# Memory heads' P times V at 512 columns, a pinned weight cast, and shifted loads and steps in a two-layer encoder kernel

## The chip, the core and the metric

The kernel runs on one core of one Trainium2 chip. A core has several engines that run side by side, each with its own queue of instructions: TensorE (PE in the profile; PEld is its loading of the stationary operand), VectorE (DVE), ScalarE (ACT), GpSimd (POOL) and SyncE (SP), which here issues most of the DMA transfers. Engines wait for one another through semaphores. On-chip memory has 128 partitions; matmuls write to eight banks of an accumulation memory (PSUM), each 128 x 512 fp32. The metric is the device time of one run in microseconds (us); the median of several runs counts.

## What is computed

Two layers (DEPTH = 2), sequence 512, width 2048, batch 1. Each layer normalises x, projects it, and runs three groups of heads side by side: eight heads of latent attention (MLA) over 512 keys, a short gated convolution, and four memory heads, which attend to 256 memory tokens. The outputs are gated, projected back, normalised and added to x. The parts that matter here:

```python
def memory_attention(q, mem_n, w_mk, w_mv):
    mk = (mem_n @ w_mk).reshape(b, m, MEM_HEADS, MEM_HEAD_DIM)      # 256 keys, 4 heads of 128
    mv = (mem_n @ w_mv).reshape(b, m, MEM_HEADS, MEM_HEAD_DIM)
    sc = einsum('bshd,bmhd->bhsm', q, mk) * MEM_HEAD_DIM ** -0.5
    p = softmax(sc, axis=-1)
    o = einsum('bhsm,bmhd->bshd', p, mv)

for l in range(DEPTH):
    z = rmsnorm(x, pre_norm_g[l]) @ w_in[l]
    q_lat, kv_lat, k_pe, gb, gc, xin, q_mem, gate = split_cols(z)
    q = rmsnorm(q_lat, ...) @ w_uq[l]            # the MLA heads' q, then rope on 64 columns
    k_nope, v = split(rmsnorm(kv_lat, ...) @ w_ukv[l])
    a_out = mla_attention(q, k, v)
    c_out = short_gated_conv(gb, gc, xin, conv_w[l])
    m_out = memory_attention(q_mem, rmsnorm(mem, ...), w_mk[l], w_mv[l])
    o = (concat(a_out, c_out, m_out) * silu(gate)) @ w_o[l]
    x = x + rmsnorm(o, post_norm_g[l])
```

## The kernel before

**Products in three parts.** Every fp32 operand is split into a high half, rounded to the matmul's own 32-bit type, and a low half, the rest. `mm3` (lines 267 to 269) makes a product of three matmuls: high times high, high times low, low times high. `split_to` (272 and 273) makes the halves of a result: ScalarE copies it (the cast), VectorE subtracts.

**Weights.** `Program` keeps a list of steps; a step names the weight units that it reads. A unit is loaded by SP into one of eight raw buffers (`wr`) and prepared in two instructions: a ScalarE cast to `wh` (184) and a VectorE subtraction to `wl` (185), each in one of three buffers. With `parts=2` each is done in two halves, so that the first half is there sooner. Loads are issued some eight units ahead, preparations two units ahead of their step.

**What sets the order.** TensorE, GpSimd and SP run in the order in which the program was written. ScalarE and VectorE are ordered by the framework's scheduler, except in the first stretch of the kernel, up to the memory keys of layer 1, where they too keep program order.

**The start.** Layer 1 begins with the memory tokens' keys and values: sixteen steps (`mem_steps`) that alternate keys and values for eight slices `kp` of the width, 256 rows of `w_mk` or `w_mv` each. The operands `mH`, `mL` are the memory tokens, transposed ahead of time. Twelve matmuls on ones (`warm(12)`, line 1372) stand ahead of them. The table `beside` names what else is put behind each of the sixteen steps: loads of x rows (`xr[t][0]`), their squares (`xr[t][1]`), loads of the transposed x (`load`), and its multiplications by the norm's gains on ScalarE (`gain`, line 687). All loads are on SP's queue.

**The mixer.** `mixer` runs the heads of a layer. Each head has four steps, one for each 128 queries: `score` (three matmuls, the row maximum on VectorE at 1126, the exponential on ScalarE at 1129, reciprocal at 1131, normalised P on ScalarE at 1132), `trans` (TensorE transposes at 1142 to `ptp`, then a cast and a subtraction to the halves of `PT`), and `av`, the product of P and V into `o`. `pipeline` writes them out: step k issues `score` of iteration k, then what `between` holds for k, then `trans` of iteration k - 3, and `av` of iteration k - 5 (k - 4 for the whole MLA heads). The four memory heads come first (iterations 0 to 15), then four pairs of MLA heads. In an MLA head `av` runs once, 512 queries wide, with the slabs `PTh` and `PTl`. In a memory head it runs twice, for 256 queries each, from a slab `PT` for each half:

```python
if t % 2 == 0:
    st["PT"] = slab("PT", F32R).rearrange("p (s k c) -> p s k c", s=2, k=4)
...
o = st["o"] if whole else st["o"][:, b * 256:(b + 1) * 256]
```

**Between.** `qkv_steps` are the six projections that a pair of MLA heads needs: two of q (`qps`), two of k (`kps`), two of v (`vps`); the weight units are `uq` and `ukv`. `spread` distributes the six over the steps of the heads that run before that pair: the first pair's over the sixteen steps of the memory heads, another pair's over the eight steps of the pair before it, save that those of the fourth pair are put within six of the third pair's eight steps. `pair2` holds what is added in the third pair: `use_y` and two casts of gated outputs y, `low(0)` and `low(1)`, at steps 6, 6 and 7.

Of the kernel before, what the change touches and what calls it, by code (L numbers as in the profile page):

```python
# [5 lines left out]
F32 = mybir.dt.float32  # L6
F32R = mybir.dt.float32r
# [56 lines left out]
class Unit:  # L64
# [5 lines left out]

    def __init__(self, key, loads=None, more=None, sums=(), then=(), place=None, alloc=None, gain=None, parts=1, behind=None):
        self.key = key
        self.loads = loads or {}
        self.more = more
        self.sums, self.then = sums, then
        self.place = place
        self.alloc = alloc
        self.gain = gain
        self.parts = parts
        self.behind = behind  # L80


class Program:
    def __init__(self, nc, raw, hi, lo, ahead=2, loads_ahead=6, more_ahead=5):
        self.nc = nc
        self.pools = raw, hi, lo
        self.ahead, self.loads_ahead, self.more_ahead = ahead, loads_ahead, more_ahead
        self.steps = []
        self.early = 0
        self.queue = []  # L90
# [32 lines left out]
    def run(self):  # L123
# [39 lines left out]
        def prep(upto):  # L163
            while at["prep"] < min(upto, len(seq)):
# [5 lines left out]
                u = seq[c]  # L170
                src = tiles[u.key]
                for a, b in u.sums:
                    nc.vector.tensor_tensor(tiles[a], tiles[a], tiles[b], op=ALU.add)  # L173
# [7 lines left out]
                if u.gain is None:  # L181
                    for k in range(u.parts):
                        h = slice(k * n // u.parts, (k + 1) * n // u.parts)
                        nc.scalar.copy(hi[:, h], src[:, h])  # L184
                        nc.vector.tensor_tensor(lo[:, h], src[:, h], hi[:, h].bitcast(F32), op=ALU.subtract)  # L185
                else:
                    gains = u.gain()
                    for k, g in enumerate(gains):
                        h = slice(k * (n // len(gains)), (k + 1) * (n // len(gains)))
                        nc.scalar.activation(hi[:, h], src[:, h], AF.Copy, scale=g)  # L190
                        nc.vector.scalar_tensor_tensor(lo[:, h], src[:, h], g, hi[:, h].bitcast(F32),
                                                       op0=ALU.mult, op1=ALU.subtract)
# [30 lines left out]
def encoder(tc, x, xt, mem, memt, positions, columns, w_in, q_norm_g, w_uq, w_qr, kv_norm_g, w_ukv,  # L223
# [18 lines left out]
    dram = pool("dram", space=bass.MemoryType.DRAM)  # L242
    pr = Program(nc, raw_p, hi_p, lo_p)
    add = pr.add
# [539 lines left out]
    def mem_steps(l):  # L784

        def unit(name, w, kp):
            if (l, kp) == (0, 0):
                return Unit((name, l, kp), {(name, l, kp): [w[j * P:(j + 1) * P, :] for j in range(2)]}, parts=2)
            return Unit((name, l, kp), {(name, l, kp): [w[kp * 256:(kp + 1) * 256, :].rearrange("(a p) c -> p a c", p=P)]})

# [252 lines left out]
    def qkv_steps(l, pair, st):  # L1043
# [3 lines left out]
        qu = Unit(qk, {qk: [wl[:, :, 2 * pair + i, :NOPE] for i in range(2)]})  # L1047
        ku = Unit(kk, {kk: [wkv[:, :, pair * 512:(pair + 1) * 512]]})

# [48 lines left out]
    def head_iters(j, rope, src, keys, whole=False):  # L1098
# [4 lines left out]
        def room(t):  # L1103
            if whole:
                if t == 0:
                    st["PT"] = [slab(n, F32R).rearrange("p (k c) -> p k c", k=kts) for n in ("PTh", "PTl")]
                sl = slice(t * P, (t + 1) * P)
                return [a[:, :, sl] for a in st["PT"]]
            if t % 2 == 0:
                st["PT"] = slab("PT", F32R).rearrange("p (s k c) -> p s k c", s=2, k=4)  # L1110
            sl = slice((t % 2) * P, (t % 2 + 1) * P)
            st["PT", t // 2] = [st["PT"][:, s, :kts] for s in range(2)]
            return [a[:, :, sl] for a in st["PT", t // 2]]
# [32 lines left out]
        def av(b):  # L1146
            def g():
# [10 lines left out]
            return g  # L1158
        return [((score(t), [], 0.4), trans(t), av(t // 2) if t == 3 or t == 1 and not whole else None, 4 if whole else 5)
                for t in range(NT)]  # L1160
# [10 lines left out]
    def mem_head(i):  # L1171
        def src():
# [3 lines left out]
                    (lambda k: V[:, 0, k, ds], lambda k: V[:, 1, k, ds]))  # L1176
        return head_iters(12 + i, None, src, MT)

# [24 lines left out]
    def mixer(l, C, gates, pair2, tail):  # L1203
# [16 lines left out]
        for pair in range(4):  # L1220
            for i in range(2):
                its += mla_head(2 * pair + i, sts[pair])
            nxt = tail if pair == 3 else spread(6 if pair == 2 else 8, qkv_steps(l, pair + 1, sts[pair + 1]),
                                                0.0 if pair else 0.25)
# [171 lines left out]
    add(row_load("x", x[0], 0))  # L1396
    add(lambda: warm(12))
    G["src"], G["dst"] = x[0], None
    for l in range(depth):
# [7 lines left out]
        if l == 0:  # L1407
# [20 lines left out]
            def load(h, g):  # L1428
# [4 lines left out]
            beside = {  # L1433
                0: [xr[1][0]], 2: [load(0, 0)], 4: [xr[0][1]], 5: [xr[1][1], load(0, 1)],
                6: [wide_of(0), gain(0, 0, 0, 2)], 7: [gain(0, 0, 2, 6)], 8: [gain(0, 0, 6, 8), row_of(0)],
                9: [scaled(0, 0, 0), gain(0, 1, 0, 4), mr[0][0]], 10: [left_part(0, 0, 0)],
# [116 lines left out]
        if l + 1 < depth:  # L1553
            add(lambda: G.update(mTd=dram.tile([4, P, D], F32, name="mTd")))
        mixer(l, C, gates, {6: [(use_y, []), (low(0), [])], 7: [(low(1), [])]}, last_pair)
        add(sums(1))
# [56 lines left out]
```

## Time and profile before

| | |
|---|---|
| median of 3 runs | 1476.92 us (1476.54 to 1476.97) |
| profiled execution, its own time | 1476.71 us |
| its span in the trace | 1474.9 us |
| mean granted TensorE clock | 0.999 |
| DMA | 288.93 MB, mean 196 GB/s |
| longest group by line | ScalarE's weight casts, line 184: 434 instructions, 445.4 us |

The span runs from the first to the last recorded instruction; the execution's own time is 1.8 us longer. In the profile's rows of a timeline stand start, duration, engine, line, operation, output and inputs, shape, count, and in brackets the idle time before the instruction with what ended it. In rows of groups the numbers behind the first bar are the busy time in us and the mean duration in ns, behind the second the idle time. In rows by windows, the window and its length come first, then the busy us and the number of instructions of PE, PEld, DVE, ACT and POOL, the granted clock, the DMA share and GB/s. Matmuls overlap in their pipeline: the duration of one is longer than the time from its start to the next one's.

### The profile page before, as it was taken

How to read it: one execution, taken by the hardware profiler on the slowest of the kernel's cores; microseconds unless marked ns; L12 is line 12 of the kernel's file. 1: busy time of each engine (PE TensorE's matmuls, PEld its weight loads, DVE VectorE, ACT ScalarE, POOL GpSimd, SP SyncE). 2: the span in 40 equal slices, each digit the busy share in tenths (PEclk: the TensorE clock that was granted, in tenths of full speed). 3: DMA queues.
4: the chain of work that ended last, by engine and by line, in shares of the span. 5: the costliest groups of instructions: out<-in, count | busy, mean ns of one | idle time of the engine just before them, and what ended most of it. 6: DMA issues, size and time to landing. Idle time of an engine off the chain costs nothing.

```text
span 1474.9 us, 19573 instructions
## 1 busy us (share of the span) xinstructions
PE 1462.4 (99%) x7250; PEld 1251.1 (85%) x7250; DVE 1087.8 (74%) x1442; ACT 863.9 (59%) x1314; POOL 269.0 (18%) x276
## 2 busy tenths in 40 slices
PE   9999999999999999999999999999999999999997
PEld 8888888899888888888898888888988888888886
DVE  5899677957557778868789666776575677688687
ACT  7856343446459688654777434434464686786443
POOL 0032302032301010321220333030322000003111
PEclk9999999999999999999999999999999999999999
DMA  9999979697964292695986999695979554128945
GB/s 359 402 268 225 212 193 187 168 190 218 210 198 107 74 278 84 126 227 152 344 290 228 237 231 228 185 177 162 212 203 210 169 135 104 41 87 151 263 114 186
DMA packets 142512, 288.93 MB, mean 196 GB/s; under 512 B 9872, under 2 KB 32656, under 8 KB 138576
## 3 DMA queue, kind: packets, MB, share of 16 engines
q0 software_dynamic: 56576, 129.51, 43.3%
q1 hardware_dynamic: 85840, 158.16, 32.6%
q8 instruction: 57, 0.93, 0.3%
q14 instruction: 39, 0.32, 0.1%
HBM read 266.01 MB, written 21.63 MB: 195 GB/s over the span
## 4 chain that ended last, share of the span: by engine, by line
PE 94%; ACT 2%; DVE 2%; DMA 2%; issue 0%; SPq 0%; DVEq 0%; POOLq 0%; ACTq 0%
PE P L268 23%; PE P L267 23%; PE P L269 23%; PE ptp L1142 2%; PE tps L884 2%; PE o L268 1%; PE o L269 1%; PE o L267 1%; PE sc L268 1%; PE sc L267 1%; PE sc L269 1%; PE mk L269 1%; PE sc L1123 1%; PE sc L1124 1%; DMA wr<-in_w_mk_dram 1%; PE mk L268 1%
## 5 line engine op out<-in xcount | busy, mean ns | idle before, releaser
L184 ACT CAST wh<-wr 128x1024 fp32r<-128x1024 f32 (+2 forms) x434 | 445.4, 1028 | 460.9 <-PE P L269 366.4
L185 DVE TENSOR_TENSOR wl<-wr,wh 128x1024 fp32r<-128x1024 f32 (+2 forms) x434 | 516.7, 1192 | 265.3 <-ACT wh L184 258.3
L267 PE MATMUL P<-wh,S 128*128 128x512 f32 (+1 forms) x896 | 345.2, 385 | 0.0
L268 PE MATMUL P<-wl,S 128*128 128x512 f32 (+1 forms) x896 | 343.8, 384 | 0.0
L269 PE MATMUL P<-wh,S 128*128 128x512 f32 (+1 forms) x896 | 343.2, 383 | 0.0
L267 PE MATMUL P<-wh,A 128*128 128x512 f32 (+1 forms) x656 | 253.0, 386 | 0.0
L268 PE MATMUL P<-wl,A 128*128 128x512 f32 (+1 forms) x656 | 251.7, 384 | 0.4 <-DVE wl L185 0.4
L269 PE MATMUL P<-wh,A 128*128 128x512 f32 (+1 forms) x656 | 251.5, 383 | 0.0
L142 POOL DMA_DIRECT2D wr<-in_w_in_dram x132 | 158.3, 1200 | 439.0 <-DVE wl L185 324.5
L269 PEld LDWEIGHTS P<-wh,S 128*128 128x128 f32 x896 | 168.2, 188 | 30.3
L268 PEld LDWEIGHTS P<-wl,S 128*128 128x128 f32 x896 | 168.2, 188 | 29.7 <-DVE wl L185 0.3
L267 PEld LDWEIGHTS P<-wh,S 128*128 128x128 f32 x896 | 168.1, 188 | 29.8
L269 PEld LDWEIGHTS P<-wh,A 128*128 128x128 f32 x656 | 123.1, 188 | 22.4
L268 PEld LDWEIGHTS P<-wl,A 128*128 128x128 f32 x656 | 123.2, 188 | 22.2 <-DVE wl L185 0.9
L267 PEld LDWEIGHTS P<-wh,A 128*128 128x128 f32 x656 | 123.1, 188 | 21.9 <-ACT og L575 0.2
L142 POOL DMA_DIRECT2D wr<-in_w_o_dram x40 | 48.5, 1236 | 300.7 <-DVE wl L185 299.8
L1129 ACT ACTIVATE P<-sc,nm 128x512 f32<-128x512 f32 (+1 forms) x96 | 59.6, 622 | 27.6 <-DVE nm L1126 27.4
L1132 ACT ACTIVATE P<-P,rec 128x512 f32<-128x512 f32 (+1 forms) x96 | 61.6, 656 | 8.9 <-DVE rec L1131 8.9
L1126 DVE TENSOR_REDUCE nm<-sc 128x1 f32<-128x512 f32 (+1 forms) x96 | 56.7, 594 | 7.4 <-PE sc L1124 4.4
L1142 PE MATMUL ptp<-identr,P 128*128 128x128 f32 x320 | 46.1, 273 | 0.8 <-ACT P L1132 0.8
L173 DVE TENSOR_TENSOR wr<-wr,wr 128x1024 f32<-128x1024 f32 (+1 forms) x36 | 42.3, 1178 | 5.0 <-DMA wr<-in_w_in_dram 4.5
L1142 PEld LDWEIGHTS ptp<-identr,P 128*128 128x128 f32 x320 | 37.9, 140 | 6.9 <-ACT P L1132 1.2
(318 smaller groups left out, 2092.0 us busy)
## 6 DMA issues: line engine op xcount, KB each, us to landing
wr<-in_w_in_dram SPq DMA_DIRECT2D x128, 512.0 KB, 5.3
wr<-in_w_in_dram POOLq DMA_DIRECT2D x108, 512.0 KB, 7.3
wr<-in_w_o_dram SPq DMA_DIRECT2D x48, 512.0 KB, 6.3
wr<-in_w_o_dram POOLq DMA_DIRECT2D x40, 512.0 KB, 6.8
wr<-in_w_in_dram SPq DMA_DIRECT2D x32, 416.0 KB, 3.6
wr<-in_w_in_dram POOLq DMA_DIRECT2D x24, 416.0 KB, 5.6
wr<-in_w_mk_dram SPq DMA_DIRECT2D x15, 512.0 KB, 8.8
wr<-in_w_mv_dram SPq DMA_DIRECT2D x15, 512.0 KB, 10.4
```

The costliest lines, as they stand in the source:

```text
L142: engine.dma_start(dst, src, **kw)
L173: nc.vector.tensor_tensor(tiles[a], tiles[a], tiles[b], op=ALU.add)
L184: nc.scalar.copy(hi[:, h], src[:, h])
L185: nc.vector.tensor_tensor(lo[:, h], src[:, h], hi[:, h].bitcast(F32), op=ALU.subtract)
L267: nc.tensor.matmul(ps, ah, bh, start=first, stop=False, **kw)
L268: nc.tensor.matmul(ps, ah, bl, start=False, stop=False, **kw)
L269: nc.tensor.matmul(ps, al, bh, start=False, stop=last, **kw)
L884: nc.tensor.transpose(ps[:, t * P:(t + 1) * P], view(t)[:, j * P:(j + 1) * P], G["ident"])
L1126: nc.vector.tensor_reduce(nmax, ps, axis=AX.X, op=ALU.max, negate=True)
L1129: nc.scalar.activation(pt, ps, AF.Exp, bias=nmax, accum_out=tot)
L1132: nc.scalar.activation(pt, pt, AF.Copy, scale=rec)
L1142: nc.tensor.transpose(ps[:, k * P:(k + 1) * P], pt[:, k * P:(k + 1) * P], G["ident"])
```

## The change

Seven edits, all in order and shape; the arithmetic stays.

1. The memory heads become whole: `mem_head` passes `True`, one slab `PT` holds both halves for all 512 queries, and `av` runs once for each head, five steps behind as before.
2. `Unit` gets `pinned`: its cast and subtraction keep their place in program order. Only the second pair's `ukv` weight is pinned.
3. The weights of the second slice (`kp` = 1, layer 1) are prepared in two halves, as those of the first already were.
4. In `beside`, the second row load of x and the first load of transposed x come a step later, and the eight gains of that part come as 4 and 4 (behind steps 7 and 8) instead of 2, 4 and 2 (6, 7, 8).
5. `warm(12)` becomes `warm(10)`.
6. The fourth pair's projections are spread over eight steps of the third pair instead of six.
7. `use_y` and `low(0)` move from step 6 to step 3 of the third pair.

```diff
 class Unit:
-    def __init__(self, key, loads=None, ..., parts=1, behind=None):
+    def __init__(self, key, loads=None, ..., parts=1, behind=None,
+                 pinned=False):
...
+                pin = self.pin if u.pinned else lambda ins: ins
...
-                        nc.scalar.copy(hi[:, h], src[:, h])
-                        nc.vector.tensor_tensor(lo[:, h], src[:, h], hi[:, h].bitcast(F32), op=ALU.subtract)
+                        pin(nc.scalar.copy(hi[:, h], src[:, h]))
+                        pin(nc.vector.tensor_tensor(lo[:, h], src[:, h], hi[:, h].bitcast(F32), op=ALU.subtract))
...
-    pr = Program(nc, raw_p, hi_p, lo_p)
+    pr = Program(nc, tc.keep_in_program_order, raw_p, hi_p, lo_p)
...
-            return Unit((name, l, kp), {(name, l, kp): [w[kp * 256:(kp + 1) * 256, :].rearrange("(a p) c -> p a c", p=P)]})
+            return Unit((name, l, kp), {(name, l, kp): [w[kp * 256:(kp + 1) * 256, :].rearrange("(a p) c -> p a c", p=P)]},
+                        parts=2 if (l, kp) == (0, 1) else 1)
...
-        ku = Unit(kk, {kk: [wkv[:, :, pair * 512:(pair + 1) * 512]]})
+        ku = Unit(kk, {kk: [wkv[:, :, pair * 512:(pair + 1) * 512]]}, pinned=pair == 1)
...
-                if t == 0:
+                if t == 0 and kts == 2:
+                    two = slab("PT", F32R).rearrange("p (s k c) -> p s k c", s=2, k=kts)
+                    st["PT"] = [two[:, s] for s in range(2)]
+                elif t == 0:
                     st["PT"] = [slab(n, F32R).rearrange("p (k c) -> p k c", k=kts) for n in ("PTh", "PTl")]
...
-        return [((score(t), [], 0.4), trans(t), av(t // 2) if t == 3 or t == 1 and not whole else None, 4 if whole else 5)
+        return [((score(t), [], 0.4), trans(t), av(t // 2) if t == 3 or t == 1 and not whole else None, 4 if whole and kts > 2 else 5)
...
-        return head_iters(12 + i, None, src, MT)
+        return head_iters(12 + i, None, src, MT, True)
...
-            nxt = tail if pair == 3 else spread(6 if pair == 2 else 8, qkv_steps(l, pair + 1, sts[pair + 1]),
+            nxt = tail if pair == 3 else spread(8, qkv_steps(l, pair + 1, sts[pair + 1]),
...
-    add(lambda: warm(12))
+    add(lambda: warm(10))
...
-                0: [xr[1][0]], 2: [load(0, 0)], 4: [xr[0][1]], 5: [xr[1][1], load(0, 1)],
-                6: [wide_of(0), gain(0, 0, 0, 2)], 7: [gain(0, 0, 2, 6)], 8: [gain(0, 0, 6, 8), row_of(0)],
+                1: [xr[1][0]], 3: [load(0, 0)], 4: [xr[0][1]], 5: [xr[1][1], load(0, 1)],
+                6: [wide_of(0)], 7: [gain(0, 0, 0, 4)], 8: [gain(0, 0, 4, 8), row_of(0)],
...
-        mixer(l, C, gates, {6: [(use_y, []), (low(0), [])], 7: [(low(1), [])]}, last_pair)
+        mixer(l, C, gates, {3: [(use_y, []), (low(0), [])], 7: [(low(1), [])]}, last_pair)
```

How the built program's instructions stand before and after, at three places (line numbers of the changed kernel are 3 to 8 higher). SP's queue in the first stretch, before (`wr` is a raw weight buffer, `rows` a row block of x, `X` a part of transposed x):

```order
L142 DMA wr_137<-in_memt_dram 128x512
L657 DMA rows_191<-in_x_dram 128x2048
L142 DMA wr_193<-in_w_mk_dram 128x2x512
L142 DMA wr_211<-in_w_mv_dram 128x2x512
L142 DMA wr_213<-in_memt_dram 128x512
L652 DMA X_247<-in_xt_dram 128x2048
L142 DMA wr_249<-in_w_mk_dram 128x2x512
```

and after:

```order
L145 DMA wr_135<-in_memt_dram 128x512
L145 DMA wr_189<-in_w_mk_dram 128x2x512
L661 DMA rows_209<-in_x_dram 128x2048
L145 DMA wr_211<-in_w_mv_dram 128x2x512
L145 DMA wr_213<-in_memt_dram 128x512
L145 DMA wr_249<-in_w_mk_dram 128x2x512
L656 DMA X_267<-in_xt_dram 128x2048
```

The row load and the load of transposed x each moved behind one key weight, the fourth and the fifth. TensorE in the first memory head of layer 1, before, from its fourth step's transposes (`ptp`; `sc` are scores, `o` is the head's output):

```order
L1142 MATMUL ptp_3955<-identr,P_3878 128x128 x2
L267 MATMUL o_3960<-PT_3884,Vm_3707 128x256
L268 MATMUL o_3960<-PT_3884,Vm_3707 128x256
L269 MATMUL o_3960<-PT_3884,Vm_3707 128x256
...
L267 MATMUL sc_3967<-Km_3705,QmH_3572 128x256
...
L1142 MATMUL ptp_4006<-identr,P_3913 128x128 x2
L267 MATMUL o_3960<-PT_3932,Vm_3707 128x256
L268 MATMUL o_3960<-PT_3932,Vm_3707 128x256
L269 MATMUL o_3960<-PT_3932,Vm_3707 128x256
```

and after:

```order
L1150 MATMUL ptp_3956<-identr,P_3880 128x128 x2
L271 MATMUL sc_3961<-Km_3707,QmH_3574 128x256
...
L1150 MATMUL ptp_4000<-identr,P_3915 128x128 x2
L271 MATMUL o_4005<-PT_3886,Vm_3709 128x512
L272 MATMUL o_4005<-PT_3886,Vm_3709 128x512
L273 MATMUL o_4005<-PT_3886,Vm_3709 128x512
```

The six matmuls of the first half are gone from behind the fourth transposes, and the six that stood two steps later, behind the second transposes of the next head, are 512 wide. ScalarE in the memory heads, before (`wh_4259` is the second pair's `ukv` weight, `Q` the first pair's q):

```order
L1132 ACTIVATE P_3839<-P_3839,rec_3842 128x256
L1132 ACTIVATE P_3851<-P_3851,rec_3854 128x256
L184 CAST wh_4259<-wr_3581 128x1024
L272 CAST Q_3817<-qps_3857 128x512
L1129 ACTIVATE P_3878,tot_3879<-sc_3872,nm_3876 128x256
```

and after, the same place and then the place of that weight's cast (now `wh_4239`):

```order
L1140 ACTIVATE P_3841<-P_3841,rec_3844 128x256
L1140 ACTIVATE P_3853<-P_3853,rec_3856 128x256
L276 CAST Q_3819<-qps_3859 128x512
L276 CAST PT_3886<-ptp_3887 128x2x128
...
L1140 ACTIVATE P_4231<-P_4231,rec_4234 128x512
L188 CAST wh_4239<-wr_3583 128x1024
L188 CAST wh_4243<-wr_3601 128x1024
L276 CAST Q_4247<-qps_4248 128x512
```

The cast left the first memory head's steps and now stands ahead of the second pair's first q, behind all memory heads. On TensorE, in the third pair, the second k projection and both v projections for the fourth pair now stand a step later each; GpSimd's order is unchanged.

More of the change, by code (lines that the diff above doesn't have):

```diff
@@ L64, with __init__ @@
 class Unit:
-    def __init__(self, key, loads=None, more=None, sums=(), then=(), place=None, alloc=None, gain=None, parts=1, behind=None):
+    def __init__(self, key, loads=None, more=None, sums=(), then=(), place=None, alloc=None, gain=None, parts=1, behind=None,
+                 pinned=False):
         self.key = key
@@ L80, in __init__ @@
         self.behind = behind
+        self.pinned = pinned
 class Program:
-    def __init__(self, nc, raw, hi, lo, ahead=2, loads_ahead=6, more_ahead=5):
+    def __init__(self, nc, pin, raw, hi, lo, ahead=2, loads_ahead=6, more_ahead=5):
         self.nc = nc
+        self.pin = pin
         self.pools = raw, hi, lo
```

## Prediction

> **What bounds the kernel now.** First the page's table of busy times, which also says where a gain can come from.
>
> ```profile
> PE 1462.4 (99%) x7250; PEld 1251.1 (85%) x7250; DVE 1087.8 (74%) x1442; ACT 863.9 (59%) x1314; POOL 269.0 (18%) x276
> PE 94%; ACT 2%; DVE 2%; DMA 2%; issue 0%; SPq 0%; DVEq 0%; POOLq 0%; ACTq 0%
> ```
>
> The second row is the chain of work that ended last. TensorE sets the time nearly throughout, so a part of this change is worth only what it takes off TensorE's own work, or off one of the places where TensorE waits. Next I read TensorE's timeline there: first the weights of the first memory keys (a row is start, duration, instruction, and in brackets idle time and releaser).
>
> ```profile
> 1.44 5.44 PE L1372 MATMUL warm<-ones 128*128 128x512 f32 x12 [1.44 <-DVE ones L288]
> 6.72 0.28 PE L267 MATMUL mk<-mH,wh 128*128 128x256 f32 x1
> 6.95 0.28 PE L269 MATMUL mk<-mH,wl 128*128 128x256 f32 x1
> ...
> 12.45 0.28 PE L268 MATMUL mk<-mL,wh 128*128 128x256 f32 x1
> 13.20 0.39 PE L269 MATMUL mk<-mH,wl 128*128 128x256 f32 x1 [0.46 <-DVE wl L185]
> ...
> 24.66 0.28 PE L268 MATMUL mk<-mL,wh 128*128 128x256 f32 x1
> 25.70 0.39 PE L269 MATMUL mk<-mH,wl 128*128 128x256 f32 x1 [0.76 <-DVE wl L185]
> ```
>
> From 6.72 to 6.95 two 256-wide matmuls start, 0.115 us each; I use 0.12. Between 12.45 and 13.20 lie 0.75, so 0.63 is waiting; the matmul behind a wait also starts 0.10 late (454.32 to 454.54 below, 0.22 for 0.12): 0.73 us lost. Between 24.66 and 25.70 likewise 0.92 + 0.10 = 1.02. Both wait for wl, the low half of a weight, from VectorE.
>
> The second place is the memory heads of layer 1, where ScalarE is nearly full (busy us of PE, PEld, DVE, ACT, POOL in two stretches), with TensorE's rows there.
>
> ```profile
> 443.70:456.20 12.50, 12.09 (x74) 10.41 (x72) 10.58 (x24) 12.00 (x31) 3.69 (x6) 1.00 0.69 194
> 456.20:470.30 14.10, 14.10 (x110) 13.35 (x108) 11.47 (x36) 13.61 (x44) 0.00 (x0) 1.00 0.52 71
> ```
>
> ```profile
> 454.07 0.36 PE L267 MATMUL o<-PT,Vm 128*128 128x256 f32 x1
> 454.32 0.39 PE L268 MATMUL o<-PT,Vm 128*128 128x256 f32 x1
> 454.54 0.28 PE L269 MATMUL o<-PT,Vm 128*128 128x256 f32 x1
> 454.66 0.29 PE L267 MATMUL o<-PT,Vm 128*128 128x256 f32 x1
> ...
> 455.26 0.28 PE L269 MATMUL sc<-Km,QmL 128*128 128x256 f32 x1
> 455.94 0.44 PE L1142 MATMUL ptp<-identr,P 128*128 128x128 f32 x2 [0.41 <-ACT P L1132]
> ...
> 461.40 0.36 PE L267 MATMUL o<-PT,Vm 128*128 128x256 f32 x1
> 461.60 0.28 PE L268 MATMUL o<-PT,Vm 128*128 128x256 f32 x1
> ...
> 463.14 0.38 PE L1142 MATMUL ptp<-identr,P 128*128 128x128 f32 x2
> 463.27 0.36 PE L267 MATMUL o<-PT,Vm 128*128 128x256 f32 x1
> 463.63 0.39 PE L268 MATMUL o<-PT,Vm 128*128 128x256 f32 x1
> ```
>
> The second matmul behind transposes starts 0.20 after the first where nothing waits (461.40 to 461.60). Over that, 454.32 lost 0.05 and the next 0.10; 455.94 lost 0.68 - 0.12 = 0.56 waiting for ScalarE's normalised P; 463.63 lost 0.16, and I add 0.10 for the one behind it as at 454.32. Together 0.97 us, and a layer later the same pattern stands:
>
> ```profile
> 1187.02 0.44 PE L1142 MATMUL ptp<-identr,P 128*128 128x128 f32 x2 [0.41 <-ACT P L1132]
> ```
>
> The third is the third MLA pair, in each layer once:
>
> ```profile
> 556.81 0.39 PE L267 MATMUL o<-PTh,V 128*128 128x512 f32 x1
> 557.36 0.50 PE L268 MATMUL o<-PTl,V 128*128 128x512 f32 x1 [0.16 <-DVE PTl L273]
> 557.70 0.39 PE L269 MATMUL o<-PTh,V 128*128 128x512 f32 x1
> 557.93 0.39 PE L267 MATMUL o<-PTh,V 128*128 128x512 f32 x1
> ```
>
> ```profile
> 1288.43 0.50 PE L268 MATMUL o<-PTl,V 128*128 128x512 f32 x1 [0.16 <-DVE PTl L273]
> ```
>
> A 512-wide matmul takes 0.23 from start to start (557.70 to 557.93). The waits are 0.55 - 0.23 = 0.32, and 0.34 - 0.23 = 0.11 behind it: 0.43 us.
>
> **The wider P times V.** Per head and product, 12 matmuls 256 wide become 6 matmuls 512 wide. The group's row gives this for one of the three:
>
> ```profile
> L267 PE MATMUL o<-PT,Vm 128*128 128x256 f32 x32 | 10.2, 318 | 0.0
> ```
>
> By such means (318 ns here, 0.39 us for a wide one) the edit would save 12 x 0.318 - 6 x 0.39 = 1.5 us a head, 12 us in all. But the rows at 454.54 and 454.66 are 0.28 long and start 0.12 apart: durations overlap. By starts it is 12 x 0.12 - 6 x 0.23 = 0.06 a head; with 227 ns for the wide one (the rows read to two digits) 0.08. I take 0.31 us a layer. The Trainium skill says the same in "Perfetto Trace Analysis", section "Identifying the Most-Contended Engine": matmul busy time is a poor measure of how near the limit TensorE is, since pipelined matmuls overlap. By the means the sum would be some 12 us larger; the trace's starts agree with the page, and they decide.
>
> The edit also moves work. The first half's product (6 x 0.12 = 0.72 us) leaves the step of its own and joins the second half's, two steps later. TensorE therefore reaches the next scores and transposes 0.72 earlier, where ScalarE, with 0.50 and 0.49 us free in the two stretches, has no more speed to give. Scores, exponentials, casts and subtractions keep their number and width.
>
> **The pinned weight.** It takes one cast from ScalarE and one subtraction from VectorE out of the memory heads:
>
> ```profile
> 450.31 1.05 ACT L184 CAST wh<-wr 128x1024 fp32r<-128x1024 f32 x1
> ```
>
> The next ScalarE row starts at 451.26, so 0.95 us of ScalarE come free ahead of the wait at 455.94, more than its 0.56. The cast reappears behind the memory heads, ahead of the second pair's first Q cast; its first reader stands here:
>
> ```profile
> 482.43 0.39 PE L267 MATMUL kps<-ckv,wh 128*128 128x512 f32 x1
> ```
>
> The heads end near 470, so cast and subtraction (1.05 and 1.23) have about 10 us: I cost it at nothing, or 2.28 us a layer if that cover were gone.
>
> With it the 0.97 should vanish. What is late next is the merged product of the second head: it needs the fourth P's transpose cast (ScalarE) and subtracted (VectorE).
>
> ```profile
> 463.74 0.39 ACT L272 CAST PT<-ptp 128x256 fp32r<-128x256 f32 x1
> ```
>
> ```profile
> 464.29 0.41 DVE L273 TENSOR_TENSOR PT<-ptp,PT 128x256 fp32r<-128x256 f32 x1
> ```
>
> Transposes at 463.14 are ready as low half at 464.70, 1.56 later, behind exponentials and row maxima. Between transposes and merged product TensorE has two scores and two pairs of transposes, 2 x (0.44 + 0.13) = 1.1 us: a wait of 0.4, with 0.10 behind it 0.5 us. Behind the waiting matmul stand all later scores. The other heads have K projections or MLA scores, over 1 us more, in that place, so they should not wait. The bounds of this new wait are 0 and 0.97 + 0.31 = 1.28 a layer (all given back); near the latency row I take 0.6. Memory heads: 2 x (0.97 + 0.31 - 0.6) = 1.36 us gained, bounds 0 and 2 x 1.28 = 2.56, and a loss only by the slower rival below.
>
> **The start.** Two warm-up matmuls fewer free 2 x 0.44 (5.28 / 12). Then the weights' rows decide:
>
> ```profile
> 5.88 0.69 DVE L185 TENSOR_TENSOR wl<-wr,wh 128x512 fp32r<-128x512 f32 x1
> 7.30 1.34 DVE L185 TENSOR_TENSOR wl<-wr,wh 128x512 fp32r<-128x512 f32 x2 [0.72 <-ACT wh L184]
> ...
> 11.92 1.23 DVE L185 TENSOR_TENSOR wl<-wr,wh 128x1024 fp32r<-128x1024 f32 x1 [1.02 <-ACT wh L184]
> ```
>
> The first wl is there at 6.57 instead of its use at 6.95, the second half's at about 7.97 against a use near 8.15: the warm-up is worth 0.1 to 0.4. In halves, the wl of 11.92 comes about 12.1 instead of 13.15 (half a cast of 0.6 behind the load at 10.83, then 0.69), ahead of its reader: 0.73. The row load that moves behind the fourth key weight on SP's queue is 1 MB, twice a weight:
>
> ```profile
> 23.34 1.05 ACT L184 CAST wh<-wr 128x1024 fp32r<-128x1024 f32 x1 [1.44 <-DMA wr<-in_w_mk_dram]
> ```
>
> ScalarE idled 1.44 for that weight; it now lands about 2 us sooner: 1.02 more. Gross some 2 us. But this isn't kept:
>
> ```profile
> 32.00:54.00 22.00, 22.00 (x143) 20.09 (x143) 20.35 (x23) 21.19 (x31) 0.00 (x0) 1.00 1.04 396
> ```
>
> ```profile
> 35.42 1.23 DVE L185 TENSOR_TENSOR wl<-wr,wh 128x1024 fp32r<-128x1024 f32 x1 [0.20 <-ACT wh L184]
> ```
>
> ```profile
> 37.53 0.28 PE L269 MATMUL mk<-mH,wl 128*128 128x256 f32 x1
> ```
>
> From 32 to 54 us ScalarE is full, and its number of casts and gains ahead of this weight is the same as before (2, 4, 2 gains become 4, 4), so the wl of 36.65 comes no sooner. TensorE can come 0.88 earlier and then waits; less 0.05 from wl's end to its reader (13.15 to 13.20) and 0.10 behind the wait, 0.75 stays. Bounds 0 (ScalarE waits for the later X and pushes its casts back) and 0.85.
>
> **The third pair** loses its 0.43 in each layer: the second K projection, both V projections and the casts of y leave the step whose PTl was late. No work is removed, so the bounds are 0 (another PTl is late) and 0.86; I take 0.86, since elsewhere in the same pair nothing waits. The moved use_y and its casts run on ScalarE where the K and V casts stood.
>
> **Sum.** 0.75 + 1.36 + 0.86 = 2.97 us off the profiled run's own 1476.71: 1473.74. The median of the runs lies 0.21 above that run, so 1473.95; I say 1473.9.
>
> **Rivals.**
> One gain is given back (ScalarE's backlog takes the memory heads' 1.36, or X the start's 0.75): 1474.7 to 1475.3. For it: 12.00 of 12.50 and 13.61 of 14.10 busy. Against: the cast leaves ahead of the largest wait.
>
> Slower: every merged product waits for its fourth P, since it now holds back both halves. The other gains are 0.75 + 0.86 + 2 x 1.28 = 4.2, so it turns slower once each of 8 waits is over 0.53; by 1.56 - 1.1 it is 0.5 for bare steps. More than 0.2% slower takes (4.2 + 2.95) / 8 = 0.9 each. With half of another P's cast and subtraction ahead, (0.39 + 0.41) / 2, each is 0.9 and the time 1476.92 + 7.2 - 4.2 = 1479.9; with a whole one 1.3 and 1483.1. Against it: K or V projections or wide scores stand in that place for three heads of four.
>
> The clock stays low: the warm-up's 512-wide matmuls take 0.44 each, against 0.23 at 557.70; full speed came at most 5.28 us after the first. If the pause before 6.57 starts that over, 5.28 us at half pace lose 2.64, of which the vanished 2 us of waits cover most: start +0.6 instead of -0.75, 1475.3. The Trainium skill ("TensorE: Matmul & The Clock Gate", "Part 1: The HAM clock gate") has full speed after a busy window of about 3.4 us whose phase runs free; by it the loss would be about half of 3.4, 1.7 us (an estimate). The trace only shows that 12 matmuls sufficed.
>
> The pin or the spread changes nothing (the wait has another cause): each keeps its wait, 1474.8 to 1475.3, part of the first rival.
>
> **Chances.** Forecast 0.62 (1472.2 to 1474.6, about three quarters of it under 1473.97), a gain given back 0.22, slower 0.10, clock 0.06. A measurement tells 0.2%, 2.95 us: faster than that 0.48, within 0.42, slower 0.10. The low end of the range is the sum without new waits, 4.2 us: 1472.7, and 1 us for what the rows don't show; the high end takes in the given-back cases and the edge of the slower one: 1471.6 to 1476.8.
>
> **What would show it.** Right: no wait at the fourth key weight, and a new wait at the sixth's wl near 36.7; no wait for P in the second head; one at the second head's merged product, under 1 us; none at 557. Wrong: waits of over 0.5 at every merged product, casts of the pinned weight still running when kps of the second pair is due, or mk rows 0.23 apart after 6 us.

## The result, and the profile after

| | before | changed |
|---|---|---|
| median of 22 runs each | 1477.21 us (1476.31 to 1482.8) | 1474.57 us (1473.05 to 1476.54) |
| ratio, 95% interval | | 0.998 (0.9973 to 0.9986) |
| profiled execution | 1476.71 us | 1476.28 us |
| span in its trace | 1474.9 us | 1474.5 us |

The changed kernel is 2.6 us faster in the medians; 2.97 us was the forecast. The profiled executions lie off their medians, that of before 0.5 us below its own (1477.21) and that of the changed kernel 1.7 us above, so the two are only 0.43 us apart. Where in the program it stands ahead and where it lost that again is therefore the first thing to read. I take the same matmul in both traces and subtract its start times: the first weight matmul of layer 1's projection is at 54.38 before and 52.81 after, so TensorE is 1.57 us ahead there.

Three places answer to the rows shown of before. First the start, TensorE's timeline of the changed kernel (start, duration, instruction, idle and releaser):

```profile
23.59 0.28 PE L272 MATMUL mk<-mL,wh 128*128 128x256 f32 x1
24.00 0.39 PE L273 MATMUL mk<-mH,wl 128*128 128x256 f32 x1
...
35.48 0.28 PE L272 MATMUL mk<-mL,wh 128*128 128x256 f32 x1
35.86 0.39 PE L273 MATMUL mk<-mH,wl 128*128 128x256 f32 x1
```

The wait of 0.92 at the fourth key weight is 0.41 - 0.12 = 0.29 now, the one near 13 us is gone, and the forecast wait at the sixth key's wl has come, 0.26 long. So far the start did better than its sum. Then, far behind it:

```profile
137.73 0.39 PE L271 MATMUL P<-wh,S 128*128 128x512 f32 x1
138.62 0.50 PE L272 MATMUL P<-wl,S 128*128 128x512 f32 x1 [0.51 <-DVE wl L189]
...
144.63 0.50 PE L272 MATMUL P<-wl,A 128*128 128x512 f32 x1 [0.24 <-DVE wl L189]
...
148.16 0.50 PE L272 MATMUL P<-wl,A 128*128 128x512 f32 x1 [0.51 <-DVE wl L189]
```

Three waits of layer 1's projection for a weight's low half. Before has only the last of them, at 148.06. By 150 us the lead of 1.57 is gone: the matmul that stands at 150.23 before is at 150.37.

The second head's merged product in layer 1, TensorE, then ScalarE beside it:

```profile
461.76 0.38 PE L1150 MATMUL ptp<-identr,P 128*128 128x128 f32 x2
462.27 0.50 PE L271 MATMUL o<-PT,Vm 128*128 128x512 f32 x1
462.86 0.50 PE L272 MATMUL o<-PT,Vm 128*128 128x512 f32 x1
463.20 0.39 PE L273 MATMUL o<-PT,Vm 128*128 128x512 f32 x1
```

```profile
460.93 0.56 ACT L276 CAST V<-vps 128x512 fp32r<-128x512 f32 x1
461.39 0.48 ACT L1137 ACTIVATE P<-sc,nm 128x256 f32<-128x256 f32 x1
461.76 0.20 ACT L1137 ACTIVATION_READ_ACCUMULATOR P<-sc,nm 128x1 f32 x1
461.85 0.37 ACT L276 CAST PT<-ptp 128x256 fp32r<-128x256 f32 x1
```

There is no wait for P at the second head any more. In its place the product stands 0.51 behind the first of two transposes (0.14 in the first head, which waits for nothing), its second matmul 0.59 behind the first (0.31 there), the third 0.34 (0.23). That is 0.37 + 0.28 + 0.11, about 0.76 us: the cast of the last PT begins at 461.85, behind a V cast and an exponential, and VectorE's subtraction follows it. The third pair, where 557.36 waited:

```profile
556.65 0.39 PE L271 MATMUL o<-PTh,V 128*128 128x512 f32 x1
556.88 0.39 PE L272 MATMUL o<-PTl,V 128*128 128x512 f32 x1
557.11 0.39 PE L273 MATMUL o<-PTh,V 128*128 128x512 f32 x1
```

These three start 0.23 apart, so that wait is gone.

### The profile page after: what moved, and what is told of

It reads as the page before. It is cut to its first block, busy times and chain, and to the rows that moved or that the text cites. A ratio compares the mean times of both kernels' runs of the same rounds, so it can differ in the third digit from the quotient of the medians.

```text
span 1474.5 us, 19492 instructions
## 1 busy us (share of the span) xinstructions
PE 1462.4 (99%) x7200; PEld 1247.7 (85%) x7200; DVE 1087.1 (74%) x1444; ACT 862.3 (58%) x1316; POOL 269.1 (18%) x276
## 4 chain that ended last, share of the span: by engine, by line
PE 83%; DMA 7%; issue 5%; POOL 3%; DVE 1%; ACT 1%; SPq 0%; POOLq 0%; DVEq 0%; ACTq 0%
PE P L272 19%; PE P L273 19%; PE P L271 19%; DMA wr<-in_w_in_dram 3%; POOL wr L145 3%; PE ptp L1150 2%; PE tps L889 2%; DMA rows<-in_x_dram 2%; PE o L272 1%; PE o L273 1%; PE sc L272 1%; PE sc L271 1%; PE sc L273 1%; PE o L271 1%; PE sc L1131 1%
```

## The experiments

Each kernel is the kernel before with some of the edits, or the changed kernel with one more; all were timed beside runs of the kernel before on the same chip.

**The three groups apart.** `start_only` is edits 3, 4 and 5:

```diff
+                        parts=2 if (l, kp) == (0, 1) else 1)
-                0: [xr[1][0]], 2: [load(0, 0)], ...
+                1: [xr[1][0]], 3: [load(0, 0)], ...
-    add(lambda: warm(12))
+    add(lambda: warm(10))
```

> Only the edits of the start (weights of the second slice in halves, later loads of x rows and transposed x, gains as 4 and 4, ten warm-up matmuls). Theory A (a floor of transfers: the 16 DMA engines are full up to about 138 us, so the weights read between 138 and 149 us land no earlier, and what the start gains is waited away there): TensorE is 1.4 to 1.9 us ahead at 40 us, waits of about 2 us stand between 138 and 149 us where before had 0.7, and the time is 0 to 0.5 us below before. Theory B (the floor is only the noise of one run): the lead of 1.4 us stays, time 1.0 to 1.7 us below. My prediction's own reason: 0.75 below.

`heads_only` is edits 1 and 2:

```diff
+        ku = Unit(kk, {...}, pinned=pair == 1)
+        return head_iters(12 + i, None, src, MT, True)
```

> Only the wide P times V of the memory heads and the pinned weight. By the changed kernel's profile, which gained 0.34 and 0.36 us over the two layers' heads: 0.7 us below before in the medians, with a wait of 0.5 to 0.8 us at the second head's merged product and none for P. By the prediction's sum: 1.36 below. If the heads' gain in layer 1 is also waited away by transfers in layer 2: 0.3 to 0.4 below.

`third_only` is edits 6 and 7:

```diff
-            nxt = tail if pair == 3 else spread(6 if pair == 2 else 8, ...
+            nxt = tail if pair == 3 else spread(8, ...
-        mixer(l, C, gates, {6: [(use_y, []), (low(0), [])], 7: ...
+        mixer(l, C, gates, {3: [(use_y, []), (low(0), [])], 7: ...
```

> Only the spread over eight steps and the earlier use_y and low(0). As predicted: the wait for PTl near 557 and 1288 us is gone, 0.43 us a layer, 0.86 below before. If transfers in layer 2 take back what layer 1 gains: 0.4 to 0.5 below.

| kernel | median | before | ratio (95%) |
|---|---|---|---|
| start_only | 1476.56 | 1477.28 | 0.9999 (0.999 to 1.0008) |
| heads_only | 1475.96 | 1477.28 | 0.999 (0.9981 to 0.9999) |
| third_only | 1476.05 | 1477.28 | 0.999 (0.9981 to 0.9999) |

The ratios are taken over all runs and are not the quotients of the medians (that would be 0.9995 for start_only). Heads and third pair are faster, by intervals that end just under 1; the start by itself isn't told from no change, nor from the forecast 0.75 us. In its trace TensorE is 1.53 us ahead at 54 us, loses 1.0 of it here, and is 0.33 ahead at 150:

```profile
83.12 0.39 PE L267 MATMUL P<-wh,A 128*128 128x512 f32 x1
84.25 0.50 PE L268 MATMUL P<-wl,A 128*128 128x512 f32 x1 [0.73 <-DVE wl L185]
```

1.13 - 0.23 = 0.90, and 0.10 behind it. Theory A's amount is right; its place is not, since at 148 there is only the wait that before has too. What holds TensorE up at 84 us begins earlier, on ScalarE, where a weight's cast waits for its load. In before, ScalarE's cast and VectorE's wl are these:

```profile
76.72 1.05 ACT L184 CAST wh<-wr 128x1024 fp32r<-128x1024 f32 x1 [1.65 <-PE P L269]
```

```profile
82.96 1.22 DVE L185 TENSOR_TENSOR wl<-wr,wh 128x1024 fp32r<-128x1024 f32 x1
```

and in start_only, with VectorE's wait for ScalarE in between, and GpSimd's first adding load at the end:

```profile
76.74 1.05 ACT L184 CAST wh<-wr 128x1024 fp32r<-128x1024 f32 x1 [2.81 <-DMA wr<-in_w_in_dram]
```

```profile
78.12 0.43 DVE L273 TENSOR_TENSOR Km<-ks,Km 128x256 fp32r<-128x256 f32 x1 [1.38 <-ACT Km L272]
...
82.98 1.22 DVE L185 TENSOR_TENSOR wl<-wr,wh 128x1024 fp32r<-128x1024 f32 x1
```

```profile
87.22 1.25 POOL L142 DMA_DIRECT2D wr<-in_w_in_dram  x1 [5.70 <-DMA wr<-in_w_in_dram]
```

With TensorE 1.5 us ahead this cast starts no sooner, and neither does what follows it on VectorE, up to the wl at 82.98 (82.96 before) that the wait at 84.25 is for. All six profiles of kernels with the start's edits have ScalarE wait 1.8 to 2.8 us for a load near 76 us, and no other has; TensorE lost between nothing and 1.0 us to it. The two other groups gained 0.46 and 0.28 us (heads, layers 1 and 2) and 0.46 in each layer (third pair), and layer 2 took nothing back.

**What takes the start's lead.** From 87 to 128 us GpSimd issues weight loads that add to what lies in the tile. `plain_loads` lets them overwrite:

```diff
-            move(nc.gpsimd, tiles[u.key], 0, u.more, accum_op=ALU.add)
+            move(nc.gpsimd, tiles[u.key], 0, u.more)
```

> The kernel before, but GpSimd's second load of a weight overwrites the tile instead of adding to it (so sums of weights are left out of the computation; bytes, issues and waits stay). Adding transfers moved 196 GB/s with the DMA engines full (100 to 120 us), plain ones 401 GB/s (60 to 80 us). If the waits at 138 to 149 us are a floor of transfers: no wait over 0.2 us there, and the time 0.5 to 1.0 us below before. If the wait there has another cause (ScalarE or VectorE order): it stays, time as before.

`plain_start` is that with the edits of the start.

> The same overwriting loads, with the edits of the start. If the floor of transfers took the start's gain: with it lifted the gain stays, 0.5 to 1.6 us below the kernel of plain_loads (the wait near 84 us, before the adding transfers begin, may still take up to 1.0 us of it). If the gain is lost for another reason: within 0.3 us of plain_loads.

Medians 1475.98 and 1474.78 beside 1476.9 of before; ratios 0.9992 (0.9983 to 1.0001) and 0.9984 (0.9975 to 0.9992). The windows view (busy us of PE, PEld, DVE, ACT, POOL, the clock, the DMA engines' busy share, GB/s), of before:

```profile
100.00:120.00 20.00, 20.00 (x90) 16.53 (x90) 20.00 (x20) 11.43 (x12) 8.91 (x8) 1.00 1.12 196
140.00:150.00 10.00, 9.55 (x42) 7.55 (x41) 8.85 (x11) 4.50 (x6) 0.00 (x0) 1.00 0.77 247
```

and of plain_loads:

```profile
100.00:120.00 20.00, 20.00 (x90) 16.58 (x89) 19.99 (x20) 11.16 (x12) 4.97 (x7) 1.00 0.62 188
140.00:150.00 10.00, 10.00 (x45) 8.28 (x45) 9.19 (x12) 4.73 (x6) 0.00 (x0) 1.00 0.84 265
```

The same amount of data (196 and 188 GB/s) fills the DMA engines when it is added, share 1.12, and takes 0.62 of them when it overwrites. TensorE then has no idle time between 140 and 150, and gained 0.78 us there. With the start's edits on top the lead over plain_loads is 1.01 us at 54, 0.82 at 150 and 0.99 at the end: it stays. The two kernels' runs hardly overlap (1475.57 to 1476.47 and 1474.44 to 1475.67), so with overwriting loads the start is worth 1.20 us by the medians. The waits near 148 us belong to the adding loads: every profile with adding loads has one, and neither of the two without. That these loads are what takes the lead is less clear. The loss at 84 us comes ahead of them, and third_only, which is the kernel before up to 540 us, lost 1.10 us between 85 and 150 with no lead of the start's. In single transfers (the view of DMA issues between 100 and 150 us; the last numbers are KB each and median us to landing), before and plain_loads:

```profile
wr<-in_w_in_dram POOLq DMA_DIRECT2D x11, 512.0 KB, 7.3
```

```profile
wr<-in_w_in_dram POOLq DMA_DIRECT2D x10, 512.0 KB, 3.9
```

**Pin and wide product apart.** `wide_only` is edit 1, `pin_only` edit 2.

> Only the wide P times V of the memory heads, the second pair's weight cast where the scheduler puts it. If the pin is needed to take the wait for P away: that wait (0.56 us a layer) stays or moves to the merged product, and the time is 0 to 0.5 us below before, that is at most half of what both edits gave (1.3 us by medians, 0.83 us by the profile). If the wide product alone does it: 0.8 to 1.3 us below.

> Only the pinned weight. By the prediction the wait for P in the second memory head (0.56 us a layer) goes, as 0.95 us of ScalarE come free ahead of it: 0.6 to 1.1 us below before in two layers. If ScalarE's order there shifts so that another wait takes its place: 0 to 0.3 us below.

| kernel | median | before | ratio (95%) | heads, layers 1 and 2, by the trace |
|---|---|---|---|---|
| wide_only | 1479.72 | 1476.9 | 1.0017 (1.0009 to 1.0026) | +1.37, +1.37 us |
| pin_only | 1474.51 | 1476.9 | 0.9986 (0.9977 to 0.9994) | -1.04, -1.04 us |
| heads_only | 1475.96 | 1477.28 | 0.999 (0.9981 to 0.9999) | -0.46, -0.28 us |

The pin alone gives about what the whole change gives, and the wide product alone makes the kernel slower, which neither expectation had. The timeline of wide_only on TensorE shows the wait for P not removed but three times as long (1.27 us idle, 0.41 before), and the product's wait besides:

```profile
455.12 0.44 PE L1145 MATMUL ptp<-identr,P 128*128 128x128 f32 x2 [1.27 <-ACT P L1135]
...
463.16 0.50 PE L267 MATMUL o<-PT,Vm 128*128 128x512 f32 x1 [0.28 <-ACT PT L272]
463.69 0.50 PE L268 MATMUL o<-PT,Vm 128*128 128x512 f32 x1
```

TensorE comes to those transposes without the first half's product in front of them, 0.7 us sooner, while the weight's cast still stands ahead on ScalarE (at 449.49 there). In pin_only the second head's P V is this:

```profile
462.35 0.36 PE L271 MATMUL o<-PT,Vm 128*128 128x256 f32 x1
462.58 0.39 PE L272 MATMUL o<-PT,Vm 128*128 128x256 f32 x1
462.80 0.28 PE L273 MATMUL o<-PT,Vm 128*128 128x256 f32 x1
```

It is 0.23 to the second where 0.20 is free of waiting, and 0.22 for 0.12 behind it: 0.13 us is all that is left of the waits.

**The change without the wide product, and with it one step later.** `no_wide` takes edit 1 out of the changed kernel. `late_product` keeps it and issues the product six steps behind its score:

```diff
-  ... 4 if whole and kts > 2 else 5)
+  ... (4 if kts > 2 else 6) if whole else 5)
...
-            if 0 <= k - 5 < n and its[k - 5][3] == 5 and its[k - 5][2]:
-                add(its[k - 5][2])
+            for d in (5, 6):
+                if 0 <= k - d < n and its[k - d][3] == d and its[k - d][2]:
+                    add(its[k - d][2])
```

> The whole change without the wide P times V. If the wide product costs 0.6 us a layer next to the pin (its wait at the second head's merged product, less the 0.31 us of TensorE's work): 1.2 to 1.3 us below the changed kernel, 3.2 to 4 below before, TensorE gaining about 1.05 us a layer in the memory heads. If the parts overlap and the pinned weight alone reached the end of what can be had: the same as pin_only, 2.4 below before.

> The whole change, with the merged product of a memory head one step later (six behind its score instead of five). If the new wait is the latency of the fourth P's cast and subtraction against too little TensorE work before the product, one score and two transposes more and, in the second head, a V projection cover it: no wait over 0.2 us at the second head, 1.35 us gained a layer in the heads against 0.42, 1.5 to 1.9 us below the changed kernel. If ScalarE's backlog is the cause: the wait moves to another step and the time stays within 0.4 us of the changed kernel.

> The changed kernel itself, beside the two others on one chip: 2 to 3 us below before. If a floor of transfers varies from run to run, its waits between 84 and 149 us differ from those of its first profile, by 0.5 us or more in sum, while those in the memory heads agree within 0.1.

| kernel | median | ratio to before, 1476.88 (95%) | heads by the trace, two layers |
|---|---|---|---|
| no_wide | 1473.99 | 0.9976 (0.9967 to 0.9985) | -1.04, -1.04 us |
| late_product | 1473.92 | 0.998 (0.9971 to 0.9989) | -0.68, -0.68 us |
| changed_again | 1474.71 | 0.9985 (0.9977 to 0.9994) | -0.25, -0.44 us |

The intervals overlap, so the order of these three rests on the traces. In the memory heads the half-wide products beat both others in both layers. The later product has no wait of its own, as latency would have it, but ScalarE's backlog then shows one step earlier:

```profile
456.45 0.28 PE L273 MATMUL sc<-Km,QmL 128*128 128x256 f32 x1
456.96 0.44 PE L1150 MATMUL ptp<-identr,P 128*128 128x128 f32 x2 [0.23 <-ACT P L1140]
```

Each theory got half: 0.51 - 0.12 = 0.39 us has moved to P, and the total came out between the two. The changed kernel's second profile agrees with its first in the merged product's waits (0.37, 0.28 and 0.11 in both), and differs where the adding loads run: one wait there, at 146.71, and a lead of 1.36 us at 150 where the first profile had lost it all.

**Without the start too, and a start made later.** `pin_third` has edits 2, 6 and 7 only.

> Only the pin and the third pair's two edits; neither the wide product nor the start. If these parts add up (1.05 us a layer for the pin, 0.46 a layer for the third pair) and the start is worth nothing in the sum: 3.0 us below before, within 0.5 of no_wide. If the start still gives half a us or more where transfers allow it: 0.5 to 1 us above no_wide's place, that is 2.0 to 2.5 below before.

`warm_32` is the kernel before with more warm-up:

```diff
-    add(lambda: warm(12))
+    add(lambda: warm(32))
```

> The kernel before with 32 warm-up matmuls instead of 12: the memory keys begin about 4.6 us later (20 x 0.23), the transfers don't change. With a floor of transfers the delay is taken up by the waits it replaces, about 2.3 us at 12 to 32 us and 0.7 us at 148: 1.2 to 2 us above before. Without one, each wait moves along with TensorE: 4 to 4.6 above.

pin_third has 1473.68 beside 1477.61, ratio 0.9976 (0.9967 to 0.9985), the same ratio as no_wide: three of the seven edits reach what six reach. Its medians are 3.9 us apart, and the sum of its parts by trace is 1.02 + 0.48 + 1.00 + 0.46 = 2.96 us. warm_32 has 1479.03, ratio 1.0014 (1.0005 to 1.0023): 1.4 us for 20 more matmuls. Its time falls where the floor of transfers had it, but not for the whole reason:

```profile
10.26 0.28 PE L267 MATMUL mk<-mH,wh 128*128 128x256 f32 x1
...
146.43 0.50 PE L268 MATMUL P<-wl,A 128*128 128x512 f32 x1 [0.29 <-DVE wl L185]
149.95 0.50 PE L268 MATMUL P<-wl,A 128*128 128x512 f32 x1 [0.47 <-DVE wl L185]
```

The memory keys begin 3.5 us later, and 1.27 is left of that at 54 us, since the waits up to 32 us are gone. But the waits near 148 did not shrink; they stand there with TensorE 1.9 us behind. So this is no fixed date at which data arrive. A load is issued when a raw buffer comes free, that is after TensorE's own progress, and lands later (SP's loads in start_only by a median of 11.4 us from 60 to 90 us, 5.0 from 100 to 150); the waits can travel with TensorE, and a lead can be lost to them as well.

Leads over the kernel before, in us (negative is ahead), each the difference of the same matmul's start times:

| kernel | 54 us | 150 | 540 | 620 | 1163 | 1271 | 1455 |
|---|---|---|---|---|---|---|---|
| changed | -1.57 | +0.13 | -0.16 | -0.64 | +0.47 | +0.17 | -0.31 |
| changed_again | -1.39 | -1.36 | -1.61 | -2.07 | -1.70 | -2.14 | -2.61 |
| start_only | -1.53 | -0.33 | -0.33 | -0.33 | -0.50 | -0.50 | -0.46 |
| heads_only | -0.45 | +0.09 | -0.37 | -0.33 | -0.51 | -0.79 | -0.81 |
| third_only | -0.26 | +0.84 | +0.84 | +0.38 | +0.21 | +0.21 | -0.25 |
| wide_only | -0.79 | -0.82 | +0.55 | +0.54 | +0.51 | +1.88 | +1.87 |
| late_product | -1.40 | -0.50 | -1.18 | -1.65 | -1.80 | -2.48 | -2.95 |
| plain_loads | +0.12 | -0.66 | -0.66 | -0.65 | -0.68 | -0.67 | -0.70 |
| plain_start | -0.89 | -1.48 | -1.48 | -1.47 | -1.66 | -1.66 | -1.69 |
| pin_only | +0.25 | -0.02 | -1.06 | -1.05 | -1.21 | -2.25 | -2.25 |
| no_wide | -1.56 | +0.44 | -0.59 | -1.05 | -1.21 | -2.25 | -2.71 |
| pin_third | +0.39 | +0.41 | -0.61 | -1.09 | -1.11 | -2.11 | -2.57 |

The memory heads lie between 150 and 540 and between 1163 and 1271, the third pair between 540 and 620 and behind 1271. The first two columns also show how far single profiles can be trusted. heads_only, third_only, wide_only, pin_only and pin_third are the kernel before up to the memory heads, and yet stand between 0.79 ahead and 0.39 behind at 54 us, and between 0.82 ahead and 0.84 behind at 150. On average the five profiles with the start's edits and adding loads are 1.49 ahead at 54 us and 0.32 at 150; the six without these edits, before among them, 0.14 ahead and 0.08 behind. So a lead of more than 1 us at 54 us is the edits' work, and what is left of it at 150, 0.4 us on average, is smaller than the spread.

## Why the prediction came out as it did

The time lay within the range, 0.7 us above the forecast, and the direction was right. Part of that is luck: the heads gave less than their term, and the start's term rests on a reading that did not hold. By its steps:

**The start, 0.75 us: the effect came, its limit was misread, its size stays open.** Up to 40 us both waits were gone or cut, and a new one came at the sixth key weight. What failed first is the sentence that the wl of 36.65 comes no sooner, since ScalarE is full. In the changed kernel it ends at 34.58 + 1.23 = 35.81, and ScalarE shows why:

```profile
28.55 1.71 ACT L691 ACTIVATE X<-X,cols 128x256 f32<-128x256 f32 x4 [1.20 <-DMA X<-in_xt_dram]
```

```profile
34.58 1.23 DVE L189 TENSOR_TENSOR wl<-wr,wh 128x1024 fp32r<-128x1024 f32 x1 [1.00 <-ACT wh L188]
```

The cast of the fourth key weight starts 1.68 us sooner (21.66 for 23.34), and at the sixth half of that is left (33.51 for 34.35), ScalarE having waited 1.20 for the later X in between. So TensorE was 1.4 to 1.6 ahead, not 0.75. What failed next is that this "stays": I looked for what waits next up to 38 us, and neither at the loads near 76 us, for which nothing waited before, nor at the wait at 148 us that the kernel before has. What the start is worth in the end is not settled. Alone it measured 0.9999 of before, with an interval (0.999 to 1.0008) that holds 0.75 us as well; its medians are 0.72 apart; with pin and third pair the ratio is the same with and without it; with overwriting loads it is worth 1.20.

**The pinned weight.** 0.97 us a layer were to vanish; 1.04 did, in both layers, without a new wait for the weight (kps of the second pair came at 481.37 in pin_only, at 482.43 before). This was the best-founded term: the 0.95 us of ScalarE's time, ahead of a wait of 0.56.

**The wide product, +0.29 us a layer (a wait of 0.6 less 0.31 of work): right in kind, mis-sized.** Pin and wide product together were to gain 1.36 us in the two layers' heads; by the traces they gained 0.59 and 0.69 in the changed kernel's two profiles and 0.74 in heads_only. This is the term that clearly fell short, and the wide product is why. Against the pin alone it costs 1.04 - 0.46 = 0.58 in heads_only's first layer and 1.04 - 0.28 = 0.76 in the second. The wait is at the head, the product and the instruction that the prediction named, 0.76 instead of 0.6. The saved work is what was off: a head's two half products take 0.80 and 0.79 from their first start to the next score in pin_only, a merged one without a wait 1.47 in the changed kernel, so 0.12 less, of which 0.08 is the slow start behind transposes, which a score pays in its place. That leaves 0.04 us a head, not 0.08. The two edits were costed as one gain; apart, one is a loss that only the other hides.

**The third pair, 0.86 us: right.** The wait is gone and 0.46 us came in each layer, 0.92 in all. Its two edits were not run apart.

**Rivals.** The slower one was the mechanism of wide_only's second wait, but at one head of four, as the prediction argued against it; without the pin it made the kernel 2.8 us slower. "One gain is given back" happened to the start in some profiles (start_only lost 1.2 of its 1.53 us), through late loads. The clock rival fell: in the changed kernel's first profile only the first key rows are slow, and full pace is there by 6.99. In its second profile, where the first rows are fast, the third row stands at 6.77 too, since it waits for wl (last row below), so the slow rows cost nothing.

```profile
6.04 0.58 PE L271 MATMUL mk<-mH,wh 128*128 128x256 f32 x1
6.42 0.33 PE L272 MATMUL mk<-mL,wh 128*128 128x256 f32 x1
6.77 0.38 PE L273 MATMUL mk<-mH,wl 128*128 128x256 f32 x1
6.99 0.28 PE L271 MATMUL mk<-mH,wh 128*128 128x256 f32 x1
7.11 0.28 PE L272 MATMUL mk<-mL,wh 128*128 128x256 f32 x1
```

```profile
6.77 0.39 PE L273 MATMUL mk<-mH,wl 128*128 128x256 f32 x1 [0.22 <-DVE wl L189]
```

**What stays open.** The parts by trace (about 0.35 a layer for the heads, 0.46 a layer for the third pair) make 1.6 us, the medians 2.6, the interval 2.1 to 4.0. Half a us of the rest may be that the traces are held against a profile of before that lies 0.5 us under its median, and the other half may be the start, but no run shows either. Which transfers collide in which run was not found out. Near 925 us, in layer 2, TensorE loses 0.94 and 0.57 us in the changed kernel's two profiles and nothing in any other kernel's; ScalarE waits there 3.07 and 2.70 us for a weight load, and why that load is late only in this kernel is not known.

## What to carry to other kernels

Follow a gain at the start past every later place where an engine waits for the same stream, or would wait if it came there sooner: start_only lost its lead at 84 us, where the kernel before has no wait. Profile the same program more than once before a difference of under a microsecond is put down to an edit: here five kernels with the same first 440 us stood 1.2 us apart at 54 us. Put the edits of a change apart, also those that seem to serve one purpose: here a pin of one weight and the third pair's two edits (1473.68 us) do as well as all seven edits together, and one of the seven works against the rest. A wider matmul is priced from start to start, and with the cover that its smaller halves gave to the transposes behind them.

## What the runs showed of the hardware

A 512 KB load that adds into its tile took 7.3 us from issue to landing where one that overwrites took 3.9, and the DMA engines were busy 1.12 against 0.62 of the time at nearly the same GB/s (196 and 188): per byte an adding load took about 1.7 times the engine time.

TensorE came to full pace at a different moment in each execution, of the same kernel too; only the matmuls' starts and lengths show it, as the granted clock reads 1.00 in the windows view from the first matmul on. With 32 warm-up matmuls, seven run at half pace (0.43 us apart behind the second), and the eighth, at 4.57, at full pace: 3.1 us after the first.

```profile
1.44 3.29 PE L1372 MATMUL warm<-ones 128*128 128x512 f32 x7 [1.44 <-DVE ones L288]
...
4.57 0.39 PE L1372 MATMUL warm<-ones 128*128 128x512 f32 x1
```

In the first profile of the changed kernel all ten run at half pace, and so, by its length of 0.58 us, does the key row at 6.04; full pace comes about 5 us after the first. In its second profile the tenth starts 0.25 behind the ninth, which starts 3.6 us after the first, and the ten are over 0.41 us sooner:

```profile
1.44 4.63 PE L1380 MATMUL warm<-ones 128*128 128x512 f32 x10 [1.44 <-DVE ones L292]
```

```profile
1.44 4.22 PE L1380 MATMUL warm<-ones 128*128 128x512 f32 x10 [1.44 <-DVE ones L292]
```

The Trainium skill ("TensorE: Matmul & The Clock Gate", "Part 1: The HAM clock gate") has a busy window of about 3.4 us whose phase runs free of the program. That the moment moves between two executions of one kernel, from 3.6 to about 5 us, agrees with a free phase; the 3.1 us of the 32 matmuls are a little under the page's window.
